# Twenty-four modulation vectors made in the attention stage instead of the mixing stage

## The chip, the cores and the metric

The kernel runs on one core of a Trainium2 chip. The metric is device time in microseconds for one execution of the whole program, as the median of several executions. The core's engines are TensorE (PE, with its weight loads shown apart as PEld), VectorE (DVE), ScalarE (ACT), GpSimd (POOL) and SyncE (SP), which here only issues DMAs. Each engine works through its own queue in order.

## The reference, cut to what matters

Two post-norm layers run over 1024 latent and 128 context tokens of width 1024. Each layer first makes six modulation vectors of width 1024 from a condition vector, one set for latent tokens (`c`) and one for context tokens (`c_ctx`):

```python
mod = (jax.nn.silu(cvec) @ lp['w_mod'] + lp['b_mod'])[:, None, :]
sh1, sc1, g1, sh2, sc2, g2 = jnp.split(mod, 6, axis=-1)
h = x * (1 + sc1) + sh1
... = jnp.split(h @ lp['w_in'] + lp['b_in'], offsets, axis=-1)
a_out, mla_st = mla_mixer(...)     # 8 attention heads
m_out, ml_st = mlstm_mixer(...)    # 4 heads, matrix memory, both directions
g_out, hg_st = hgrn_mixer(...)     # 4 heads, gated linear recurrence, both directions
mix = jnp.concatenate([a_out, m_out, g_out], axis=-1) @ lp['w_out']
x = layernorm(ALPHA * x + g1 * mix, lp['ln1_g'], lp['ln1_b'])
h2 = x * (1 + sc2) + sh2
gate, up = jnp.split(h2 @ lp['w_ffn_in'], 2, axis=-1)
x = layernorm(ALPHA * x + g2 * ((jax.nn.silu(gate) * up) @ lp['w_ffn_out']), ...)
```

`sh1` and `sc1` are needed at once; `g1`, `sh2` and `sc2` only behind the output projection of the three mixers, and `g2` at the end of the layer.

## The kernel before

In the kernel the 6 x 1024 modulation values of a layer are 48 vectors of 128 values, numbered j = 0 to 47, kept for both conditions in `modfm`. Vectors 0 to 15 are `sh1` and `sc1`, 16 to 23 `g1`, 24 to 31 `sh2`, 32 to 39 `sc2`, 40 to 47 `g2`. One vector is made by `mod_gemv` (line 209): a DMA of 512 KB brings its 128 x 1024 weights, and for each of the two conditions one DVE instruction (`scalar_tensor_tensor`, line 213) multiplies them with the condition's row, which stands in all 128 partitions (`cB`), and sums along the row; the product itself goes to a scratch tile (`junk`). In the trace each of the two shows as a SCALAR_TENSOR_TENSOR and a short DVE_READ_ACCUMULATOR. `mod_init` loads the two rows by a broadcasting DMA, `mod_bias` (line 220) adds the bias for eight vectors, and `gsave` (line 225) transposes eight finished vectors on PE and stores them, from where `gbcast` reads a gate row later.

A layer is four stages, run one behind the other by `run`:

- `phase_a`, the mixing stage: input projection and the two recurrences. The gated recurrence (`hgrn_setup`) works on blocks of 384 tokens; the mLSTM (`ml_gates`, `ml_states`, `mlstm`) on nine chunks of 128 tokens. `mla_prep` normalises the low-rank query and key streams and spills them.
- `phase_b`, attention: weights are split into a high and a low part, keys, values and queries of head 0 are made, then 152 steps run, 8 heads x 19 steps, of which a head has one for the context tokens and nine for each half of the latent tokens. A step is three score matmuls (lines 1182 to 1184), the exponential and the high part on ACT (1185, 1186), the low part on POOL (1187), and two steps later three matmuls with the values (1255 to 1257). Between them, two pieces per step from a list `todo`: the maxima of the next head's scores (`peak`, matmul on line 1136 and a DVE reduction on line 1137), and its keys, values and queries. In heads 6 and 7 the list has `rec` (line 1222 on), which multiplies the two recurrences' outputs with their gates (line 1229) and transposes them.
- `phase_c`, output projection and first layer norm; `phase_d`, the feed-forward.

`mm3` (lines 155 to 157) makes a product of full precision out of three matmuls of split operands, and `split` (150, 151) and `unit` (145, 146) make such operands: a cast on ACT and a subtraction on DVE or POOL.

In the kernel before, layer 0 makes its vectors 16 to 39 in `phase_a`, by `start_mod`: eight between the steps of the gated recurrence's input projection and of `mla_prep`, sixteen between the chunks of `mlstm`, with two weight buffers, two condition rows and a scratch tile of their own in each place. Vectors 40 to 47 are made in the feed-forward stage (`ffn_in`), and layer 1's 48 in layer 0's `ffn_out`. Lines 1283 to 1292, which could make vectors from 40 on in attention's last heads, do nothing, since their counter starts at 40 and runs to 40.

In layer 0 `mlstm` scales its output rows on POOL (lines 865 and 876), in layer 1 on DVE (`LG`).

The program's text doesn't fix the order on an engine alone: the tile framework plans it with a model of time (`schedule_with_timeline_sim=True`), takes work that stands later in the text ahead when its operands are there, and sets the semaphores. A tile's memory is taken over from earlier tiles at the same place, and the first instruction on it waits for their last use. In `phase_b` the calls `ze([P, 328])` and `ze([P, 576])` take memory that nothing uses.

## Time and profile before

| | us |
|---|---|
| median of 3 executions | 3640.34 (3639.33 to 3640.81) |
| the profiled execution | 3641.28 |
| its span, first to last instruction | 3639.5 |
| PE busy | 3405.9 (94%) |
| DVE busy | 2264.8 (62%) |
| POOL busy | 1988.8 (55%) |
| ACT busy | 1635.7 (45%) |
| mean granted clock of PE | 0.953 of full speed |

All times in the rows below are microseconds from the span's start. In a view by stretch each row has the stretch, its length, the busy time of PE, PEld, DVE, ACT and POOL with the number of instructions, the granted PE clock, the busy share of the DMA engines and GB/s. In a view of groups each row has line, engine, operation, operands with their shapes, the count, then after the bar the busy time, the mean duration in ns, and the idle time of the engine just before them with what ended it. In a timeline a row has start, duration, engine, line and operation, with idle time before it in brackets. L213 is line 213 of the kernel; a PE that is called busy may still be waiting inside, since the ends of pipelined matmuls are modelled.

### The profile page before, as it was taken

The page shows a single profiled execution, that of the slowest core. Times are in us where ns is not written, and L with a number is a line of the kernel's source. Part 1 is how long each engine was busy: PE and PEld are TensorE (multiplying, and loading weights), DVE is VectorE, ACT ScalarE, POOL GpSimd, SP SyncE. Part 2 cuts the span into 40 slices and gives each one's busy share as a digit, 9 for nine tenths or more (in the row PEclk, how much of TensorE's full clock was granted, in tenths as well). Part 3 has the DMA queues.
Part 4 walks back from the last instruction along what each step waited for, and adds up shares of the span by engine and source line. Part 5 has one row for each costly group of instructions (what it writes and reads, how often), then busy time and mean ns, then how long its engine had stood idle before and what let it go on. Part 6 is the DMA issues. An engine that isn't in the chain of part 4 may idle for free. (4 is left out here: it accounts for less than half of the span.)

```text
span 3639.5 us, 56085 instructions
## 1 busy us (share of the span) xinstructions
PE 3405.9 (94%) x20556; PEld 3034.6 (83%) x20556; DVE 2264.8 (62%) x4492; ACT 1635.7 (45%) x2877; POOL 1988.8 (55%) x1745
## 2 busy tenths in 40 slices
PE   7999987999989999999889989989999999999997
PEld 7998875776779999988689888877767899998875
DVE  6868878555674444487775678765558544443246
ACT  4264564887343333312272636577853433333211
POOL 3455566777665555401453556567863555552176
PEclk9899976999989999999999999789999999999998
DMA  6212153002352222375422021401044322224222
GB/s 244 72 40 43 39 167 100 18 21 81 121 160 85 85 85 85 111 252 179 156 79 62 30 45 34 137 25 25 22 132 139 110 73 73 73 74 139 94 99 80
DMA packets 331272, 335.77 MB, mean 92 GB/s; under 512 B 191458, under 2 KB 270386, under 8 KB 330996
## 3 DMA queue, kind: packets, MB, share of 16 engines
q1 hardware_dynamic: 330996, 332.19, 29.5%
q8 instruction: 161, 2.64, 0.3%
q14 instruction: 115, 0.94, 0.1%
HBM read 263.54 MB, written 68.56 MB: 91 GB/s over the span
## 5 line engine op out<-in xcount | busy, mean ns | idle before, releaser
L151 POOL TENSOR_TENSOR t<-t,t 128x512 fp32r<-128x512 f32 (+3 forms) x318 | 437.8, 1378 | 374.8 <-ACT t L150 374.4
L150 ACT CAST t<-t 128x512 fp32r<-128x512 f32 (+5 forms) x404 | 270.7, 673 | 698.0 <-PE bank L1449 278.7
L1449 PE MATMUL bank<-hhi,t 128*128 128x256 f32 (+1 forms) x2816 | 570.8, 295 | 12.4 <-DVE t L1349 11.5
L155 PE MATMUL bank<-hhi,t 128*128 128x384 f32 (+1 forms) x1220 | 455.1, 378 | 19.2 <-ACT t L150 5.1
L157 PE MATMUL bank<-hhi,t 128*128 128x384 f32 (+1 forms) x1220 | 460.0, 378 | 8.8 <-DVE t L151 8.8
L1449 PEld LDWEIGHTS bank<-hhi,t 128*128 128x128 f32 x2816 | 456.2, 189 | 13.6 <-ACT t L150 12.3
L156 PE MATMUL bank<-hlo,t 128*128 128x384 f32 (+1 forms) x1220 | 460.9, 378 | 4.9 <-POOL hlo L151 4.1
L1187 POOL TENSOR_TENSOR t<-t,t 128x512 fp32r<-128x512 f32 (+1 forms) x304 | 383.3, 1281 | 125.4 <-ACT t L1186 103.0
L1449 PE MATMUL bank<-t,t 128*128 128x320 f32 (+1 forms) x3168 | 434.2, 297 | 2.3 <-DVE t L1507 1.7
L1449 PEld LDWEIGHTS bank<-t,t 128*128 128x128 f32 x3168 | 427.9, 190 | 3.7 <-DVE t L1507 1.9
L1449 PE MATMUL bank<-hlo,t 128*128 128x320 f32 (+1 forms) x1408 | 415.2, 295 | 0.0
L155 PE MATMUL bank<-t,hhi 128*128 128x256 f32 (+3 forms) x1232 | 386.8, 315 | 12.1 <-DVE t L1107 5.4
L156 PE MATMUL bank<-t,hhi 128*128 128x256 f32 (+3 forms) x1232 | 388.0, 315 | 4.3 <-POOL t L146 4.3
L157 PE MATMUL bank<-t,hlo 128*128 128x256 f32 (+3 forms) x1232 | 388.4, 316 | 0.3 <-POOL hlo L151 0.3
L155 PEld LDWEIGHTS bank<-hhi,t 128*128 128x128 f32 x1220 | 237.9, 196 | 57.3 <-ACT t L150 6.7
L1137 DVE TENSOR_REDUCE t<-bank 128x1 f32<-128x384 f32 (+1 forms) x400 | 203.9, 538 | 122.6 <-PE bank L1136 119.5
L157 PEld LDWEIGHTS bank<-hhi,t 128*128 128x128 f32 x1220 | 240.1, 197 | 39.2 <-DVE t L151 12.1
L156 PEld LDWEIGHTS bank<-hlo,t 128*128 128x128 f32 x1220 | 239.6, 196 | 34.7 <-POOL hlo L151 5.1
L1449 PEld LDWEIGHTS bank<-hlo,t 128*128 128x128 f32 x1408 | 265.4, 188 | 0.3 <-issue 0.2
L155 PEld LDWEIGHTS bank<-t,hhi 128*128 128x128 f32 x1232 | 239.8, 195 | 30.2 <-DVE t L1107 5.6
L213 DVE SCALAR_TENSOR_TENSOR t<-t,t 128x1024 bf16<-128x1024 f32 x176 | 239.3, 1359 | 40.6 <-DMA t<-in_w_mod_dram 31.6
L156 PEld LDWEIGHTS bank<-t,hhi 128*128 128x128 f32 x1232 | 240.4, 195 | 20.1 <-POOL t L146 4.7
(355 smaller groups left out, 7329.1 us busy)
## 6 DMA issues: line engine op xcount, KB each, us to landing
t<-in_w_mod_dram SPq DMA_DIRECT2D x96, 512.0 KB
t<-in_w_ffn_in_dram SPq DMA_DIRECT2D x88, 512.0 KB
t<-in_w_ffn_out_dram SPq DMA_DIRECT2D x44, 512.0 KB
t<-in_w_in_dram SPq DMA_DIRECT2D x40, 512.0 KB
shid<-t SPq DMA_DIRECT2D x88, 160.0 KB
sx<-t SPq DMA_DIRECT2D x27, 512.0 KB
t<-sx SPq DMA_DIRECT2D x27, 512.0 KB
shid<-t SPq DMA_DIRECT2D x88, 128.0 KB
```

The costliest lines, as they stand in the source:

```text
L150: self.nc.scalar.copy(hi, src)
L151: (eng or self.nc.gpsimd).tensor_tensor(lo, src, hi.bitcast(F32), op=ALU.subtract)
L155: mm(ps, a[0], b[0], start=first, stop=False)
L156: mm(ps, a[0], b[1], start=False, stop=False)
L157: mm(ps, a[1], b[0], start=False, stop=last)
L213: nc.vector.scalar_tensor_tensor(junk, raw, 1.0, cB[s], op0=ALU.mult, op1=ALU.mult, accum_out=self.modfm[:, l, j, s:s + 1])
L1137: V.tensor_reduce(nm[:, i, b:b + 1] if i < 8 else nm[:, i, 3:4], ps, axis=AX.X, op=ALU.max, negate=True)
L1187: G.tensor_tensor(pl, e, ph.bitcast(F32), op=ALU.subtract)
L1449: mm(ps, a[x][:, k * P:(k + 1) * P], view(y, k, n0, n1), start=first and k == 0 and i == 0, stop=k == 3 and i == 2, skip_group_check=True)
```

## The change

Vectors 16 to 39 of layer 0 are made in `phase_b` of layer 0 and no longer in `phase_a`: from step 3 to step 95 of attention, one after every fourth step. There is one weight buffer (`rv`), which layer 0 alone allocates. The two condition rows take two tiles of 128 x 1024, and the rings `rr` and `rg` of `rec` become four slices of 256 of the same two tiles (before: three tiles of 256 each). The scratch tile takes the place of `ze([P, 576])`, till now unused. To make room, the two one-row tiles for the softmax denominators become rows 0 and 32 of one tile. `start_mod` and the lines that did nothing go.

```diff
-    def start_mod(self, z, j0, j1):
-        raw = z.ring(2, [P, U])
-        cB, junk = [z([P, D]), z([P, D])], z([P, D], BF16)
-        self.mod_init(cB)
-
-        def gen():
-            for j in range(j0, j1):
-                self.mod_gemv(0, j, cB, raw.next(), junk)
-                if j % 8 == 7:
-                    self.mod_bias(0, j - 7, 8)
-                if j == 23:
-                    self.gsave(0, 16, self.r_m.next())
-                yield
-
-        return gen()
...
-                        bg = self.start_mod(Zone(self, c, "gemv"), 16, 24) if l == 0 else iter(())
+                        bg = iter(())
...
-                bg = self.start_mod(zl, 24, 40) if l == 0 else iter(())
+                bg = iter(())
...
-            ze([P, 576])
+            junk = ze([P, 576]).bitcast(BF16)[:, 0:D]
...
-            rdn = z.ring(2, [1, QB])
-            rr, rg = z.ring(3, [P, 256]), z.ring(3, [P, 256])
+            dn = z([33, QB])
+            rdn = Ring([dn[0:1, :], dn[32:33, :]])
+            cB = [z([P, D]) for _ in range(2)]
+            rr, rg = [Ring([a[:, 256 * i:256 * (i + 1)] for i in range(4)]) for a in cB]
+            if l == 0:
+                rv = z.ring(1, [P, U])
...
-            todo, gj = [], [40]
+            todo, mods = [], list(range(16, 40))
...
-                if l == 0 and n == 6 * 19 + 6 and gj[0] < 40:
-                    cB = [wks[:, i, :].bitcast(F32) for i in range(2)]
+                if l == 0 and n == 0:
                     self.mod_init(cB)
-                    junk = wqs.tiles[0].rearrange("p a b -> p (a b)").bitcast(BF16)
-                if l == 0 and n >= 6 * 19 + 7 and n%2==1 and gj[0] < 40:
-                    j = gj[0]
-                    gj[0] += 1
-                    self.mod_gemv(0, j, cB, rU.tiles[j % 2][:, 0:U], junk)
+                if l == 0 and n % 4 == 3 and mods:
+                    j = mods.pop(0)
+                    self.mod_gemv(0, j, cB, rv.next(), junk)
                     if j % 8 == 7:
                         self.mod_bias(0, j - 7, 8)
+                    if j == 23:
+                        self.gsave(0, 16, r_p.next())
```

## Rows read from the trace of the kernel before

**Rows 1.** The page: busy time per engine, and 40 slices of the span.

```profile
PE 3405.9 (94%) x20556; PEld 3034.6 (83%) x20556; DVE 2264.8 (62%) x4492; ACT 1635.7 (45%) x2877; POOL 1988.8 (55%) x1745
...
PE   7999987999989999999889989989999999999997
...
PEclk9899976999989999999999999789999999999998
```

**Rows 2.** Busy time by stretch: from:to, length, PE, PEld, DVE, ACT, POOL, clock, DMA.

```profile
80.00:100.00 20.00, 15.07 (x86) 14.34 (x85) 20.00 (x35) 6.65 (x9) 9.01 (x6) 0.74 0.41 142
...
120.00:140.00 20.00, 14.06 (x93) 13.45 (x92) 19.96 (x50) 6.05 (x10) 16.35 (x14) 0.80 0.22 62
481.40:614.90 133.50, 95.73 (x453) 80.39 (x452) 121.04 (x329) 53.29 (x119) 94.75 (x96) 0.67 0.51 158
2287.30:2394.90 107.60, 90.00 (x454) 79.47 (x454) 91.11 (x294) 59.56 (x143) 55.10 (x65) 0.68 0.41 122
614.90:813.90 199.00, 193.58 (x943) 152.34 (x942) 109.43 (x215) 163.66 (x319) 147.68 (x121) 0.98 0.08 18
813.90:929.30 115.40, 105.43 (x475) 75.98 (x475) 67.40 (x131) 89.42 (x173) 86.43 (x67) 0.96 0.29 80
```

**Rows 3.** Busy time by stretch of line 213 alone, on DVE.

```profile
74.00:132.00 58.00, 21.08 (x32) 0.91 0.31 104
481.40:557.40 76.00, 25.38 (x37) 0.74 0.60 181
557.40:614.90 57.50, 18.96 (x28) 0.59 0.39 126
1060.00:1500.00 440.00, 26.81 (x32) 1.00 0.30 89
```

**Rows 4.** Waits, 74:140: who waited for whom, us in total, times, longest.

```profile
PE bank L156 <- POOL t L146: 4.3, 2, 3.7
PE bank L225 <- DVE modfm L220: 4.2, 1, 4.2
```

**Rows 5.** Groups by line in 481.4:614.9: count | busy us, mean ns | idle.

```profile
L213 DVE SCALAR_TENSOR_TENSOR t<-t,t 128x1024 bf16<-128x1024 f32 x32 | 44.1, 1377 | 5.7 <-DMA t<-in_w_mod_dram 3.7 <-DMA t<-scr 1.9
...
L865 POOL TENSOR_TENSOR t<-t,t 128x256 f32<-128x256 f32 x18 | 17.2, 976 | 7.5 <-DVE t L862 6.8 <-DVE modfm L220 0.5
```

**Rows 6.** Groups by line in layer 1's 2287.3:2394.9.

```profile
L876 DVE TENSOR_TENSOR t<-t,t 128x256 f32<-128x256 f32 x18 | 9.8, 551 | 0.1
...
L865 DVE TENSOR_TENSOR t<-t,t 128x256 f32<-128x256 f32 x18 | 8.1, 494 | 0.0
```

**Rows 7.** Groups by line in 614.9:813.9, layer 0's attention.

```profile
L1187 POOL TENSOR_TENSOR t<-t,t 128x512 fp32r<-128x512 f32 x90 | 116.8, 1316 | 33.7 <-ACT t L1186 29.3 <-PE bank L1257 1.6 <-ACT t L1185 1.3
L1137 DVE TENSOR_REDUCE t<-bank 128x1 f32<-128x384 f32 x115 | 60.5, 550 | 45.2 <-PE bank L1136 44.7
...
L1128 DVE CAST t<-hlo 32x1152 fp32r<-32x1152 f32 x5 | 6.8, 1355 | 1.0 <-PE bank L1182 0.8
...
L1108 DVE TENSOR_TENSOR t<-t,t 128x384 f32<-128x384 f32 x3 | 5.8, 1934 | 0.0
...
L151 DVE TENSOR_TENSOR t<-t,t 64x1152 fp32r<-64x1152 f32 x3 | 5.3, 1765 | 1.2 <-ACT t L150 1.1
```

**Rows 8.** Timeline of DVE in attention, 690:702.

```profile
695.23 4.33 DVE L1108 TENSOR_TENSOR t<-t,t 128x384 f32<-128x384 f32 x1
```

**Rows 9.** Timeline of POOL, the same stretch.

```profile
694.96 1.30 POOL L151 TENSOR_TENSOR hlo<-t,hhi 128x512 fp32r<-128x512 f32 x1
696.21 2.93 POOL L1187 TENSOR_TENSOR t<-t,t 128x512 fp32r<-128x512 f32 x3
```

**Rows 10.** Timeline of PE, the same stretch.

```profile
700.09 0.33 PE L1136 MATMUL bank<-t,t 96*128 96x128 f32 x1 [2.61 <-DVE t L1137]
```

**Rows 11.** Busy time by stretch, in layer 0's feed-forward input.

```profile
1100.00:1150.00 50.00, 50.00 (x379) 50.00 (x378) 23.83 (x38) 15.44 (x32) 31.00 (x27) 1.00 0.29 87
```

**Rows 12.** Timeline of DVE near 560: start us, duration us, line, operation.

```profile
560.55 0.63 DVE L1229 TENSOR_TENSOR t<-t,t 128x256 f32<-128x256 f32 x1
```

## The prediction

> **What bounds the kernel now.** I read the page first. The tensor engine (PE) is busy for 94% of the span [rows 1], so the kernel is bound by PE wherever PE's slice shows a 9, and work on VectorE (DVE) costs time only where PE's slice falls. The reader is to see the two kinds of place where it falls beside a lower granted clock: in slice 1, at the start, and in slices 6 and 7, where the recurrences end and attention begins and the granted clock is 7 and 6 tenths (in layer 1 that place is slices 26 and 27, at 7 and 8).
>
> Then I read busy times by stretch, with edges taken from the trace: 481.4 is the end of the last gated-recurrence output, 614.9 the first softmax exponential of attention. This stretch, which I call the transition, takes 133.5 us in layer 0 with DVE busy for 121.0 of them, PE for 95.7 at a granted clock of 0.67 [rows 2]. Layer 1 runs the same stretch without modulation vectors in 107.6 us [rows 2]. So DVE is what is late in layer 0's transition, and 25.9 us stand between the two layers.
>
> Line 213 alone says where the moved work sits. One vector is two halves, each one multiply with a sum (scalar_tensor_tensor) and one read of the accumulator: 4 instructions. The 24 moved vectors stand in two places [rows 3]: 8 of them (32 instructions, 21.1 us) in 74 to 132, and 16 in the transition, 37 instructions in its mLSTM part and 28 in its last 57.5 us (one on the edge counts twice). The other eight of layer 0's later vectors run under the feed-forward product and stay.
>
> Where the work goes, steps 0 to 95 of layer 0's attention (614.9 to 813.9), PE is busy for 193.6 of 199.0 us, POOL for 147.7, ScalarE for 163.7 and DVE for 109.4 [rows 2]. PE is the bound there, but two others are not far behind.
>
> **The change, part by part.**
>
> *Eight vectors leave the start.* DVE is busy for all of 80 to 100 and 120 to 140, where PE idles 4.9 and 5.9 us [rows 2]. Of these 10.9 us, 4.3 are PE waiting for POOL's split of a weight, line 146, which is no gemv; 4.2 are PE's transposition of the eight finished vectors (line 225), waiting for their bias [rows 4]. I take 10.9 less 4.3 = 6.6 us as the gain; ends 0 (something else is late in the same places) and 10.9 us.
>
> *Sixteen vectors leave the transition.* They take 25.4 + 19.0 = 44.3 us of DVE there [rows 3]. Without them DVE has 121.0 - 44.3 = 76.7 us of work, less than layer 1's 91.1 in 107.6 us [rows 2]. What is late next is POOL: layer 0 leaves the two row scalings of the mLSTM output on POOL (lines 865 and 876; 865 alone takes 17.2 us) where layer 1 has them on DVE at 8.1 and 9.8 us [rows 5, 6]. POOL has 94.8 us in layer 0's transition [rows 2]. So 107.6 us is the floor, a gain of 25.9, and I take 20: 113.5 us, in which POOL's 94.8 fit. The other end is 5 us, if POOL's queue is what the first attention step waits for.
>
> *Twenty-four vectors enter attention,* one after every fourth step, 3 to 95. Each brings a DMA of 512 KB on SP's queue, two DVE halves and, after each eighth, one bias. The price of a vector on DVE is 21.08 / 8 = 2.64 us at its least and 26.81 / 8 = 3.35 us beside POOL's work [rows 3], so 63 to 80 us. DVE's 109.4 + 63 = 172 us still fit into 199, and 109.4 + 80 = 189 just. Cover by count alone is there; whether it holds is the question, since DVE's queue is in order and the reductions of the score peaks (115 full ones of 0.55 us [rows 7]) that free PE's banks stand behind a gemv half.
>
> The price that decides is met in the trace at 695.23: a DVE product of two SBUF tensors, line 1108, took 4.33 us [rows 8], against a smallest share of the same form of about (5.8 - 4.33) / 2 = 0.7 us [rows 7]. POOL ran four instructions without a break from 694.96 to 699.14 [rows 9], and DVE's instruction ended right after them. PE, whose banks wait for the reduction queued behind it, stood for 2.61 us [rows 10]. A gemv half is of this kind too: two SBUF tensors in.
>
> The Trainium skill, "SBUF — State Buffer", section "Who interferes with whom", states that a DVE instruction with two SBUF inputs contends with a GpSimd instruction that reads SBUF, and that whoever has the shared ports keeps them for its whole instruction. By that rule, the trace agrees at this place (4.33 us), and it speaks against the change.
>
> As a mechanism of this kernel: if the gemv halves and POOL's instructions take turns, the 199.0 us must hold POOL's 147.7 us and 24 x 2.64 = 63.4 us one after the other, 211.1 us in all, which is 12.1 us too many. I add 2 us for half of the transposition's 4.2 us wait [rows 4], which moves here too (line 225 now takes one of the three banks of attention's ring), and take +14 us. The low end is 0: in the feed-forward product, eight vectors run beside POOL at 31.0 of 50 us and PE stays at 50.00 [rows 3, 11]. The high end is the price paid in the transition: 25.9 us for 16 vectors is 1.6 us each, 39 us for 24.
>
> *The queues that it is moved past.* SP issues 24 loads more in attention; with one buffer each waits for the gemv before. Behind it on SP stand the small round trips of the softmax sums, which are due four and more steps (8 us) later, so a wait of one gemv is covered. The DMA engines are busy for 0.08 there [rows 2]; 24 x 512 KB over 199 us is 63 GB/s beside 18. In the transition the two loads of the silu rows and sixteen of weights go away; DVE's own waits for them there were 5.7 us [rows 5], and lie within the gain.
>
> *Shared memory.* The buffers of the gated recurrences' tail (rings r and g) go from three to four entries and hold the gemv's rows until step 95; their first use in order is in head 6, step 116, so nothing waits by count. Today the first of their products runs at 560 already [rows 12], well ahead; in layer 0 this is no longer possible, and they run where PE idles 10.0 of 115.4 us [rows 2]. I take 0, within 3 us either way. The denominators now lie in one tile of two rows; a row is reused two blocks of nine steps later. Nothing.
>
> *The sum.* -6.6 - 20 + 14 = -12.6 us. The profiled execution took 3641.28 us (span 3639.5 and 1.8 around it), 0.94 above the median of 3640.34. So 3641.3 - 12.6 = 3628.7 there, and 3628 for the median.
>
> **The rivals.**
>
> *Attention hides it all.* For it: PE at 50.00 in the feed-forward stretch [rows 11], and DVE idle for 89.6 of 199.0 us [rows 2]. Against it: in the feed-forward product PE waits for DVE seldom, in attention every peak waits for a reduction. Time: 3641.3 - 26.6 - 0.9 = 3614.
>
> *The halves and POOL block each other, and PE pays as in the transition* (slower). Place: steps 0 to 95. Price: 1.6 us per vector, 39 us; -26.6 + 39 = +12.4, so 3653. It decides from 26.6 / 24 = 1.1 us per vector on; my +14 is 0.58. For it: 4.33 us and PE's 2.61 [rows 8, 10], and the sum of 211 over 199. Against it: the eleven SBUF-only instructions of the like that attention has on DVE in these steps (five casts, six products) average 1.6 us [rows 7], and PE idles only 5.4 us over all of them [rows 2].
>
> *The transition stays as long.* The kernel's order comes from a planner that pulls ready work ahead: a product that is written for head 6 stands at 560, 54 us ahead of attention's first step [rows 12]. It may pull the first new vectors back into 557 to 615, as soon as their memory is free, or POOL's 94.8 us may bound it. Gain there 5 instead of 20: -6.6 - 5 + 14 = +2.4, so 3643. The change then does only part of what it says. Against it: layer 1's 107.6 us with more DVE work than layer 0 will have [rows 2].
>
> **How the numbers follow.** Forecast 0.42 (3618 to 3638), all hidden 0.14, blocked 0.22, transition stays 0.22. A measurement of this kernel can tell about 0.2%, 7.3 us, from no change: 3633 to 3648 is "same". Faster: four fifths of the forecast, the hidden case and a little of the last, 0.49; slower: the blocked case and a quarter of the last, 0.27; same: the rest, 0.24. The likeliest is 3628. With the blocked case's 3653 and bounds of the unknown costs about it, and the hidden case's 3614, the range is 3607 to 3660.
>
> **What the changed profile would show.** Right: no line 213 between 74 and 615 but the first eight's; 80 to 140 with PE idle under 5 us; the last recurrence output to the first exponential in 110 to 118 us; steps 0 to 95 in 208 to 218 us with gemv halves above 1.4 us on average and PE waiting for line 1137 more than today's. Wrong: gemv rows ahead of the first exponential, a transition above 125 us, steps 0 to 95 within 3 us of 199 (hidden) or above 230 (blocked). Layer 1's stretches should stand within 3 us.

## The result, and the profile after

The changed kernel took 3664.23 us, median of 5 executions (3656.29 to 3670.05), beside 3640.81 (3639.33 to 3651.36) of the kernel before: a ratio of 1.0054 [1.0030, 1.0078] (ratios weigh all executions; the two medians alone would give 1.0064). Run again later (`after_again`, expected below) it took 3663.28 beside 3646.26, 1.0050 [1.0033, 1.0068]. The forecast was 3628, its range ended at 3660. The profiled execution has a span of 3667.5 us, 28.0 more than before.

The page of the changed kernel, which answers to [rows 1]:

```profile
PE 3426.9 (93%) x20556; PEld 3049.5 (83%) x20556; DVE 2283.6 (62%) x4492; ACT 1640.2 (45%) x2879; POOL 1998.2 (54%) x1745
...
PE   8999997899979999999899989989989899999997
...
PEclk9999967999989999999999999789999999999998
```

The sums hardly move; what moves is where PE idles. The first slice rises from 7 to 8. Slices 6 and 7 (455 to 637 us) stood at 8 and 7; now slices 7 and 8 (550 to 734 us) stand at 7 and 8, and those hold the end of the transition and the first two thirds of attention's steps 0 to 95. The stretches of the changed kernel, in the columns of [rows 2]. Lines have moved: 1187 is now 1175 (POOL's subtraction), 1137 is 1125 (the reduction of a peak), 1136 is 1124, 1257 is 1245 (the last product with the values), 1219 is 1207 (POOL's scaling by the softmax sums).

```profile
80.00:100.00 20.00, 17.45 (x146) 16.67 (x146) 17.13 (x33) 13.97 (x18) 11.47 (x13) 1.00 0.09 27
120.00:140.00 20.00, 20.00 (x178) 19.87 (x178) 16.07 (x65) 3.63 (x8) 8.32 (x9) 1.00 0.23 68
458.50:579.60 121.10, 101.09 (x461) 88.52 (x460) 92.41 (x279) 60.62 (x143) 83.44 (x101) 0.61 0.43 132
579.60:822.70 243.10, 213.20 (x932) 159.46 (x932) 171.83 (x300) 164.46 (x318) 172.50 (x121) 0.91 0.20 60
822.70:935.70 113.00, 101.90 (x475) 74.82 (x475) 71.40 (x131) 89.08 (x172) 87.72 (x66) 0.97 0.25 74
2304.50:2421.60 117.10, 98.85 (x454) 87.22 (x453) 95.16 (x296) 59.80 (x142) 55.30 (x65) 0.66 0.40 117
```

80 to 100 and 120 to 140 idle for 2.6 us in place of 10.9. The last gated-recurrence output comes at 458.5, not 481.4; the transition takes 121.1 us in place of 133.5; steps 0 to 95 take 243.1 in place of 199.0, which is more than both gains together; behind step 95 the stretch is 2.4 us shorter. POOL, which has the same 121 instructions there, is busy for 172.5 us in place of 147.7. Layer 1's transition takes 117.1 us in place of 107.6.

Of the 28.0 us between the two profiles only 9.8 stand at the end of layer 0's output projection (1044.1 in place of 1034.3, the start of the last instruction that takes up its products). The other 18.2 come behind it, in work that the change leaves alone; in the profile of `after_again` it is 9.0 and 17.4. The experiments on the memory come back to this.

A stretch can be split, as an estimate, by its own row: PE's busy time times the granted clock is the work at full speed, the rest of its busy time is what the clock took, and length less busy is idle. Steps 0 to 95 were 189.7 + 3.9 + 5.4 [rows 2]; now they are 194.0 + 19.2 + 29.9. The work is nearly the same; 24.5 us more are idle and 15.3 us more went with the clock.

Groups by line in that stretch, changed kernel (answering to [rows 7]):

```profile
L1175 POOL TENSOR_TENSOR t<-t,t 128x512 fp32r<-128x512 f32 x90 | 133.0, 1502 | 42.0 <-ACT t L1174 33.5 <-PE bank L1172 5.0 <-PE bank L1245 3.4
L213 DVE SCALAR_TENSOR_TENSOR t<-t,t 128x1024 bf16<-128x1024 f32 x37 | 66.7, 1801 | 23.9 <-DMA t<-in_w_mod_dram 23.8
L1125 DVE TENSOR_REDUCE t<-bank 128x1 f32<-128x384 f32 x118 | 61.7, 547 | 22.8 <-PE bank L1124 22.0
```

A half takes 1.80 us on average (1.38 in the transition before [rows 5]); 90 POOL subtractions take 1.502 in place of 1.316; and DVE stood for 23.8 us waiting for the weights of the next vector. The reductions keep their 0.55. Matched one by one in the trace, 35 of the 90 subtractions met a half and took 1.82 us on average, the other 55 took 1.30; of all 48 moved halves, nine met no POOL instruction and took 1.20 to 1.23 us, the other 39 took 1.79 on average. What PE and POOL stood for there (who waited for whom, us in total, times, longest; `sri` brings the softmax sums back by SP's queue):

```profile
PE bank L1124 <- DVE t L1125: 10.9, 6, 3.9
PE bank L1245 <- POOL t L1175: 7.6, 10, 1.5
POOL t L1175 <- ACT t L1174: 49.5, 17, 16.0
POOL t L1207 <- DMA t<-sri: 12.5, 4, 6.6
```

The two waits of PE were 2.6 and 0.3 us before. How the two slow each other, on three engines' timelines:

```profile
698.10 2.11 DVE L213 SCALAR_TENSOR_TENSOR t<-t,t 128x1024 bf16<-128x1024 f32 x1 [1.06 <-DMA t<-in_w_mod_dram]
...
700.61 1.81 DVE L213 SCALAR_TENSOR_TENSOR t<-t,t 128x1024 bf16<-128x1024 f32 x1
```

```profile
699.08 4.47 POOL L1175 TENSOR_TENSOR t<-t,t 128x512 fp32r<-128x512 f32 x2
```

```profile
701.39 0.45 PE L1245 MATMUL bank<-t,t 128*65 128x512 f32 x1 [0.85 <-POOL t L1175]
...
703.61 0.44 PE L1245 MATMUL bank<-t,t 128*65 128x512 f32 x1 [0.67 <-POOL t L1175]
```

Two subtractions next to two halves took 4.47 us, 2.2 each, and PE waited for both. That is the other direction of [rows 8 to 10], where DVE was the one held up.

### The profile page after: what moved, and what is told of

Its sections match the earlier page's. It is cut to its first block, busy times and chain, and to the rows that moved or that the text cites. A ratio compares the mean times of both kernels' runs of the same rounds, so it can differ in the third digit from the quotient of the medians.

```text
span 3667.5 us, 56098 instructions
## 1 busy us (share of the span) xinstructions
PE 3426.9 (93%) x20556; PEld 3049.5 (83%) x20556; DVE 2283.6 (62%) x4492; ACT 1640.2 (45%) x2879; POOL 1998.2 (54%) x1745
## 5 line engine op out<-in xcount | busy, mean ns | idle before, releaser
L1175 POOL TENSOR_TENSOR t<-t,t 128x512 fp32r<-128x512 f32 (+1 forms) x304 | 407.8, 1362 | 147.1 <-ACT t L1174 117.4
L213 DVE SCALAR_TENSOR_TENSOR t<-t,t 128x1024 bf16<-128x1024 f32 x176 | 255.1, 1450 | 54.2 <-DMA t<-in_w_mod_dram 51.6
```

The lines of the kernel that those rows point to most:

```text
L213: nc.vector.scalar_tensor_tensor(junk, raw, 1.0, cB[s], op0=ALU.mult, op1=ALU.mult, accum_out=self.modfm[:, l, j, s:s + 1])
L1175: G.tensor_tensor(pl, e, ph.bitcast(F32), op=ALU.subtract)
```

## The experiments

The theories: **P**, a half and POOL's instructions hold one another up; **Q**, DVE's queue is simply too full, whatever POOL does; **D**, with one weight buffer the load comes late and DVE's queue stands behind it; **S**, the loads cost by their place on SP's queue or in the DMA engines; **M**, the changed memory costs. Ratios are to the kernel before on the same chip, with 95% intervals; one per cent is 36 us.

| run | time, us | ratio | steps 0 to 95 |
|---|---|---|---|
| before | 3640 to 3646 | 1 | 199.0 |
| after_again | 3663.28 | 1.0050 [1.0033, 1.0068] | 241.9 |
| no_vectors | 3612.17 | 0.9913 [0.9890, 0.9936] | 199.4 |
| loads_only | 3601.42 | 0.9888 [0.9867, 0.9908] | 194.3 |
| one_input | 3643.29 | 0.9994 [0.9982, 1.0006] | 213.3 |
| short_loads | 3659.88 | 1.0052 [1.0033, 1.0072] | 229.0 |
| quarters | 3658.54 | 1.0040 [1.0024, 1.0057] | 235.6 |
| sixteen_moved | 3651.30 | 1.0017 [1.0003, 1.0030] | 222.6 |
| eight_moved | 3651.59 | 1.0022 [1.0006, 1.0037] | 203.6 |
| rings_only | 3648.85 | 1.0019 [1.0008, 1.0031] | 196.2 |
| after_old_rings_l1 | 3654.55 | 1.0035 [1.0021, 1.0049] | 240.6 |
| eight_old_rings_l1 | 3645.60 | 1.0005 [0.9992, 1.0018] | 205.8 |
| start_later | 3644.11 | 0.9995 [0.9984, 1.0006] | 204.3 |
| start_out | 3638.33 | 0.9989 [0.9978, 0.9999] | 209.1 |
| start_loads_only | 3640.76 | 0.9988 [0.9974, 1.0002] | 211.1 |
| start_short_loads | 3641.50 | 1.0000 [0.9992, 1.0009] | 196.4 |
| start_pinned | 3631.47 | 0.9977 [0.9962, 0.9991] | 194.5 |
| start_pinned_again | 3638.07 | 0.9977 [0.9965, 0.9990] | 194.0 |
| start_pinned_cq | 3644.63 | 0.9996 [0.9983, 1.0010] | 198.6 |

The last column is one profiled execution each, first exponential to that of step 96. Steps 0 to 95 of a kernel like before spread over 194 to 211 us there, so only differences above that say something.

**The changed kernel once more.**

> The changed kernel itself once more, beside the kernel before on this chip, so that the other runs of this group have a figure taken under the same conditions. Expected: 3655 to 3666, a ratio of 1.003 to 1.007.

As expected; in its profile, steps 0 to 95 and the subtraction's mean (1.501) repeat to 1.2 us and 0.001 us.

**What the vectors cost, and whether it is the loads.** `no_vectors`:

```diff
+        nc.vector.memset(self.modfm[:, 0, 16:40, :], 0.0)
...
-                rv = z.ring(1, [P, U])
...
-                    self.mod_init(cB)
...
-                    self.mod_gemv(0, j, cB, rv.next(), junk)
```

> The changed kernel with the 24 vectors left out wholly (no loads, no DVE halves; the values are set to zero, so layer 0's first gate and second modulation are wrong). It is the floor for all that follows. All theories expect: attention's steps 0 to 95 of layer 0 back at 199 us within 4 (243.1 in the changed kernel), DVE's transition work near 77 us and the transition at 105 to 112 us, total 3590 to 3602. If instead steps 0 to 95 stay above 215, the new rings or the shared denominators cost the time and not the vectors.

`loads_only` keeps the loads and drops the halves:

```diff
...
-                    self.mod_gemv(0, j, cB, rv.next(), junk)
+                    nc.sync.dma_start(rv.next(), ins["w_mod"][0, j])
```

> The changed kernel with the 24 loads of weights and the two rows kept, but without the DVE halves (values set to zero). Theory P (halves and POOL block each other on what they share), theory Q (DVE's queue is simply longer) and theory D (DVE's queue stands still until the late load has landed, 23.8 us in the changed kernel) all expect the floor within 5 us, since nobody waits for the loads: 3590 to 3605. Theory S (SP's queue and the transfers themselves hold up attention) expects 10 us or more above the floor.

```profile
566.90:766.30 199.40, 194.48 (x951) 151.51 (x950) 113.07 (x225) 166.15 (x323) 148.40 (x121) 0.99 0.08 18
```

That row is steps 0 to 95 of `no_vectors`: they are back at 199.4 us. Against it the changed kernel's vectors cost 1.0050 - 0.9913, 50 us, 2.1 us a vector (with both intervals some 10 us either way). The time, 3612, is 10 us above what all theories expected. With the loads alone nothing is lost (0.9888; by that floor the vectors would cost 59 us), so the loads by themselves cost nothing. But none of these loads waits for a half to free its buffer; for that part of S see `short_loads`.

**One SBUF input in place of two.** Each half becomes a plain sum of the weights, with one SBUF input and as many columns (and without the product tile that a half writes):

```diff
-                    self.mod_gemv(0, j, cB, rv.next(), junk)
+                    raw = rv.next()
+                    nc.sync.dma_start(raw, ins["w_mod"][0, j])
+                    for s in range(2):
+                        V.tensor_reduce(self.modfm[:, 0, j, s:s + 1], raw, axis=AX.X, op=ALU.add)
```

> The changed kernel with each DVE half replaced by a sum over the weight row alone (tensor_reduce, one input from SBUF instead of two, some 1.2 us like the half at its least; the product with the condition is left out). Loads, buffers and places are kept. Theory P expects POOL's subtraction (line 1175) back at 1.32 us from 1.50, the sums at 1.2 us instead of the halves' 1.80, and steps 0 to 95 at 205 to 215 us, total 3600 to 3615. Theory Q expects 235 to 245 us for these steps and 3645 to 3660 in all. Theory D expects the waits for loads to stay above 15 us and steps 0 to 95 at 222 to 232 us, total 3625 to 3640.

The durations in ns, min/median/max, of the 48 instructions of the changed kernel and of this one, then this one's steps 0 to 95 and its group of POOL's subtractions:

```profile
L213 DVE SCALAR_TENSOR_TENSOR t<-t,t x48: 1202/1528/5092, 526.4 to 727.2; 128x1024 bf16<-128x1024 f32 x48
```

```profile
L1278 DVE TENSOR_REDUCE modfm<-t x48: 1167/1209/1221, 470.0 to 642.3; 128x1 f32<-128x1024 f32 x48
```

```profile
584.20:797.50 213.30, 201.25 (x934) 154.82 (x933) 130.69 (x240) 164.74 (x320) 147.49 (x121) 0.94 0.14 39
```

```profile
L1175 POOL TENSOR_TENSOR t<-t,t 128x512 fp32r<-128x512 f32 x90 | 117.0, 1318 | 51.3 <-ACT t L1174 33.5 <-PE bank L1172 12.5 <-PE bank L1244 3.5
```

At their least the two cost the same (1.17 and 1.20 us). With one input none of 48 takes more than 1.221, though 44 of them ran beside a POOL instruction, and the 14 subtractions that met a sum took 1.28 us on average. With the matching of the changed kernel's own instructions above, it is shown that a half and POOL's instructions stretch one another: P. That it comes from the second SBUF input rather than from the product that a half writes as well, two other DVE products of the changed kernel suggest (450 to 930 us; `bank` is one of the banks that PE writes its results to, `t` lies in SBUF; ns, min/median/max):

```profile
L1095 DVE TENSOR_TENSOR t<-bank,t x12: 515/542/557, 533.7 to 700.1; 128x384 f32<-128x384 f32 x12
L1217 DVE TENSOR_TENSOR t<-t,t x18: 404/648/2248, 731.7 to 923.7; 128x256 f32<-128x256 f32 x18
```

The first has one SBUF input and writes a wider result, eleven of twelve times beside POOL, and never stretches; the second has two and does.

What the stretching costs is not isolated by this run. The planner set 29 of the 48 sums ahead of the first exponential (of the halves 11), so that 19 stand in steps 0 to 95 in place of 37; POOL's mean of 1.318 is in part that. And DVE waits there 9.0 us for weights in place of 23.8. By time the two-input form, and what moved with it, is 1.0050 - 0.9994 = 20 us of the 50; 3643 is well above the 3600 to 3615 that P forecast. The other 30 us (0.9994 - 0.9913) remain with one input: Q and D, of which the profile has 13.9 in steps 0 to 95 and 16.9 in the transition (126.1 us beside the 109.2 of `no_vectors`).

**The late load.** `short_loads` fills the buffer once and cuts the 24 loads to 32 KB (the product is made with what the buffer holds):

```diff
+                nc.sync.dma_start(rv.tiles[0], ins["w_mod"][0, 16])
...
-                    self.mod_gemv(0, j, cB, rv.next(), junk)
+                    raw = rv.next()
+                    nc.sync.dma_start(raw[:, 0:64], ins["w_mod"][0, j][:, 0:64])
...
```

> The changed kernel with the loads of the 24 vectors cut to 64 of 1024 columns (32 KB instead of 512 KB; the other columns stay those of vector 16, so layer 0's second set of values is wrong), halves and places kept. Theory D (DVE's queue stands still for a late load, 23.8 us in the changed kernel) expects these waits below 8 us and attention's steps 0 to 95 at 215 to 225 us, total 3635 to 3645. Theory P (halves and POOL block each other) expects the halves still above 1.6 us, POOL's subtraction above 1.45 us and the steps at 232 to 245 us, 3650 to 3665, unless the plan puts the halves elsewhere.

```profile
L1176 POOL TENSOR_TENSOR t<-t,t 128x512 fp32r<-128x512 f32 x90 | 132.2, 1492 | 47.3 <-ACT t L1175 34.4 <-PE bank L1173 9.2 <-PE bank L1245 3.7
...
L1279 DVE SCALAR_TENSOR_TENSOR t<-t,t 128x1024 bf16<-128x1024 f32 x34 | 61.3, 1804 | 5.7 <-DMA t<-in_w_mod_dram 5.5
```

DVE's wait for the weights falls from 23.8 to 5.5 us, halves and subtractions stay as slow (1.804, 1.492), and steps 0 to 95 shorten by 14 us (with 34 halves in them in place of 37). Yet the time doesn't fall beyond its uncertainty (1.0052 beside 1.0050), where D had forecast 3635 to 3645. D is real in the profile and small, or given back, in the time. The rest of S goes with it: SP still stands 45.3 us behind halves that hold the buffer (36.6 in the changed kernel), and POOL's wait for the softmax sums (12.5 us above, 2.3 before) is gone, without a gain in time.

`quarters` does the same product from two loads of 256 KB each in two half buffers, with 96 instructions of 512 columns:

```diff
-                rv = z.ring(1, [P, U])
+                rv, mx = z.ring(2, [P, U // 2]), z([P, 8, 2])
...
-                    self.mod_gemv(0, j, cB, rv.next(), junk)
+                    for q in range(2):
+                        raw, cs = rv.next(), slice(512 * q, 512 * q + 512)
+                        nc.sync.dma_start(raw, ins["w_mod"][0, j][:, cs])
+                        for s in range(2):
+                            V.scalar_tensor_tensor(junk[:, cs], raw, 1.0, cB[s][:, cs], ...
...
```

> The changed kernel with each vector in two loads of 256 KB into two buffers of half the size, and each half in two quarters of 512 columns (96 instructions in place of 48, the two sums added for eight vectors at once). The same product is computed. Theory D (a vector waits for its load, since there is one buffer, and the reductions of the peaks wait behind it): the loads are hidden, steps 0 to 95 take about 229 us in place of 243, 3645 to 3654. Theory P with short holds (a quarter lets a reduction in sooner, and waits for POOL only as much in all): steps 0 to 95 below 222, 3638 to 3648. Rival (each instruction waits for POOL anew, so twice as many instructions wait twice as often): quarters above 1.1 us on average, steps 0 to 95 at 243 or more, 3660 to 3675.

```profile
L1279 DVE SCALAR_TENSOR_TENSOR t<-t,t x96: 647/843/2029, 517.1 to 696.9; 128x512 bf16<-128x512 f32 x96
```

A quarter takes 0.65 us at its least and 1.03 on average, so 96 of them take 98.5 us of DVE, where the 48 halves of the changed kernel take 81.0 (58 at their least): each instruction waits anew, as the rival has it, though less at a time (it expected above 1.1 us). Steps 0 to 95 at 235.6 and 3658.54 lie between the theories, and the interval overlaps the changed kernel's: no gain is shown.

**Fewer vectors.** `sixteen_moved` leaves 16 to 23 at the start and sets 24 to 39 after every sixth step:

```diff
-                        bg = iter(())
+                        bg = self.start_mod(Zone(self, c, "gemv"), 16, 24) if l == 0 else iter(())
...
-            todo, mods = [], list(range(16, 40))
+            todo, mods = [], list(range(24, 40))
...
-                if l == 0 and n % 4 == 3 and mods:
+                if l == 0 and n % 6 == 5 and mods:
```

> The changed kernel with the vectors 16 to 23 back at the start as in the kernel before, and only 24 to 39 in attention, one after every sixth step. Theory P (a half and the POOL subtraction hold one another up, about 1.8 us a vector) gives steps 0 to 95 in 215 to 230 us, a transition of 115 to 125 us and a start as before: 3641 - 12 + 24 + 6 for the shared memory = about 3659, between 3648 and 3664. Rival Q (the loss comes from too many vectors in the 96 steps and falls away at the slower pace): steps 0 to 95 in 200 to 210 us, and 3636 to 3645.

```profile
588.50:811.10 222.60, 206.23 (x945) 158.96 (x945) 148.61 (x269) 164.76 (x320) 163.83 (x121) 0.93 0.17 47
```

222.6 us, as P has it, with 11.0 idle and 10.5 of clock more than before. `eight_moved` moves 16 to 23 alone, after every twelfth step, and `mlstm` keeps its sixteen:

```diff
-                bg = iter(())
+                bg = self.start_mod(zl, 24, 40) if l == 0 else iter(())
...
-            todo, mods = [], list(range(16, 40))
+            todo, mods = [], list(range(16, 24))
...
-                if l == 0 and n % 4 == 3 and mods:
+                if l == 0 and n % 12 == 11 and mods:
```

> Only vectors 16 to 23 move into attention, one after every twelfth step; 24 to 39 are made between the mLSTM chunks as before. In the changed kernel the start is 23 us shorter up to the last gated-recurrence output, and a vector in attention costs 44 / 24 = 1.8 us. If both hold one by one: 3641 - 23 + 8 x 1.8 = 3632. If the price is lower for vectors that stand further apart (theory P, where a half hits a POOL that has idle time in between): 0.5 us each, 3622. If the start's gain is lost again on the way (by other work that was planned behind it): 3640 or more.

There steps 0 to 95 took only 203.6 us, since the planner ran all 48 halves (16 moved, 32 of `mlstm`) between 470 and 632, 38 of them ahead of the first exponential, so that the transition stayed as long as before (134.5 us). The pace written in the text does not bind. The time is what the third expectation has (3640 or more).

**The memory.** `rings_only` is the kernel before with the new rings and the denominators' tile alone:

```diff
-            rdn = z.ring(2, [1, QB])
-            rr, rg = z.ring(3, [P, 256]), z.ring(3, [P, 256])
+            dn = z([33, QB])
+            rdn = Ring([dn[0:1, :], dn[32:33, :]])
+            cB = [z([P, D]) for _ in range(2)]
+            rr, rg = [Ring([a[:, 256 * i:256 * (i + 1)] for i in range(4)]) for a in cB]
...
```

> The kernel before with the memory part of the change alone: denominators as two rows of one tile, and the rings r and g as four slices of two shared tiles. The vectors are made where they were. In the changed kernel, and in all four variants run so far, layer 1 (whose work is the same) takes 2 to 19 us longer than in the kernel before, most of it between step 133 of attention and the end of the output projection and in the mLSTM part. Theory M (the memory part costs it): layer 1 longer by 8 to 12 us, 3648 to 3654 in all. The other theory (a shifted plan and the spread between executions, nothing of the memory): within 4 us of the kernel before.

`after_old_rings_l1` is the changed kernel with those lines for layer 0 and the old two for layer 1:

```diff
+            if l == 0:
...
+            else:
+                rdn = z.ring(2, [1, QB])
+                rr, rg = z.ring(3, [P, 256]), z.ring(3, [P, 256])
```

> The changed kernel with the shared memory in layer 0 alone; layer 1 has its three-entry rings and two denominator tiles as before. Theory M expects 8 to 12 us less than the changed kernel's 3660, so 3648 to 3652. The other theory expects 3656 to 3664.

The memory costs 0.19%, 7 us (3 to 11). The changed kernel is about as much faster without it in layer 1, but 3654.55 lies between the two expectations and its interval overlaps the changed kernel's. Where: step 133 to the end of the output projection, layer 1, in the kernel before, the changed one and `after_old_rings_l1`:

```profile
2662.80:2811.30 148.50, 142.60 (x645) 111.65 (x646) 113.86 (x194) 63.86 (x114) 63.91 (x44) 0.99 0.43 130
```

```profile
2690.40:2847.20 156.80, 146.38 (x651) 113.63 (x650) 114.99 (x194) 65.16 (x117) 64.64 (x44) 0.97 0.41 126
```

```profile
2684.80:2833.50 148.70, 141.69 (x645) 110.41 (x646) 112.67 (x194) 63.76 (x114) 65.35 (x44) 1.00 0.43 130
```

A wait for shared memory is not what does it. `start_out` below has the old memory and takes 157.2 us for this stretch, while `start_pinned` takes 148.5. Over all twenty profiles, the eight in which PE's instructions there follow each other as in the kernel before take 148.0 to 152.8 us; the twelve in which they come in another order, two of them with the old memory, take 152.9 to 158.1. The planner carries an edit in layer 0 on into layer 1's order. That the order, rather than the memory behind it, costs this stretch its 6 to 8 us is argued from these profiles; no run fixed the order alone, and the stretch is only part of what `rings_only` loses behind layer 0's output projection (13.6 us in its profile).

`eight_old_rings_l1` is `eight_moved` with the old rings in layer 1:

```diff
...
+            else:
+                rdn = z.ring(2, [1, QB])
+                rr, rg = z.ring(3, [P, 256]), z.ring(3, [P, 256])
```

> Only vectors 16 to 23 in attention, one every twelfth step, and the shared memory in layer 0 alone. With eight vectors moved, layer 0 ended 10 us earlier than in the kernel before and layer 1 took 14 us longer. Theory M expects layer 1 back and 3630 to 3634, faster than both kernels. The other theory expects 3645 to 3652 as with the shared memory in both layers.

A miss: no faster than before. It counted on the start's 22.9 us, which the next runs take apart.

**What the start was worth.** `start_later` is the kernel before without the call of `next(bg, None)` in the first projection, so that the eight vectors are written behind it.

```diff
                             V.tensor_tensor(v[:, tt, :], ps, br, op=ALU.add)
-                            next(bg, None)
```

> The kernel before, one edit: the eight vectors 16 to 23 are no longer issued one for each tile of the first value projection (74 to 132 us) but one for each of the next eight tiles, the latent projections. No vector enters attention and no memory changes. Theory A (the start was dear because the eight vectors filled VectorE in 80 to 140, which let TensorE idle and its granted clock fall to 0.74 to 0.80): the last output of the gated recurrences comes 10 to 20 us earlier than the 481.4 of before, the rest keeps its length, and the time is 3622 to 3635. Rival B (the eight vectors cost the start about their own length wherever they stand before the recurrences): 3638 to 3646, no change.

It tells nothing of A or B: the sixteen halves still ran between 74 and 130, where the planner had them. `start_out` leaves them out, `start_loads_only` keeps their loads, `start_short_loads` keeps the halves and cuts six of the loads:

```diff
+        nc.vector.memset(self.modfm[:, 0, 16:24, :], 0.0)
...
-                self.mod_gemv(0, j, cB, raw.next(), junk)
+                if j >= 24:
+                    self.mod_gemv(0, j, cB, raw.next(), junk)
```

> The kernel before with the vectors 16 to 23 left out (not computed, taken as zero ahead of their bias); all else, the memory too, as before. It gives the whole price of the eight at the start. Expected if the 22.9 us of the changed kernel's start are these vectors': the last output of the gated recurrences near 459 in place of 481, and about 3620 (3614 to 3628). If part of it came from the changed memory or order: 3628 to 3640.

```diff
...
+                else:
+                    self.nc.sync.dma_start(raw.next(), self.ins["w_mod"][0, j])
```

> The kernel before with the eight loads of 512 KB kept at the start and their sixteen halves left out (taken as zero). Theory V (the price is VectorE's 21 us of halves in front of other work): as without the vectors, 3614 to 3628, TensorE's granted clock near 1.00 in 80 to 140. Theory L (the price is the loads, which stand on SyncE's queue and in the DMA engines ahead of the weights): 3634 to 3646, and the clock in 80 to 140 as in the kernel before.

```diff
...
+                    w = raw.next()
...
+                        self.nc.sync.dma_start(w[:, 0:64], self.ins["w_mod"][0, j][:, 0:64])
...
```

> The kernel before with the sixteen halves kept at the start and six of the eight loads cut to 32 KB (the product is made with what the buffer holds). Theory V: as before, 3638 to 3646. Theory L: 3616 to 3630.

Without the eight, 80 to 140 has PE at 57.1 of 60 us:

```profile
80.00:140.00 60.00, 57.09 (x491) 55.73 (x490) 43.67 (x149) 22.49 (x34) 30.86 (x30) 1.00 0.18 50
```

Before it was 49.1 at a clock of 0.85. The first gated-recurrence output comes 25.3 us earlier (214.6 in place of 239.9), but the last one only 8.4 earlier (473.0), and layer 0's output projection ends 5.0 us earlier (1029.3 in place of 1034.3; `rings_only`, which moves no vector, has 1029.7, so this says little). By time it is 0.11% [0.01, 0.22], 4 us. So a stage boundary that comes 25 us sooner was worth 4; where the rest went is not shown. In the profiles DVE is the price, as theory V says: with the loads alone PE's clock in 80 to 140 is at 1.00, with the halves and short loads it stays at 0.85. In the time the intervals of the three (0.9989, 0.9988, 1.0000) overlap, and of the size that V gave (3614 to 3628) nothing is left.

`start_pinned` has the edit of `start_later` and ties each load behind a latent-projection tile by a one-column copy into its buffer; `start_pinned_cq` takes the query's projection, one stage later:

```diff
...
+            self.pin = y[:, 0:1]
             next(bg, None)
...
+                w = raw.next()
+                if j < 24:
+                    self.nc.vector.tensor_copy(w[:, 0:1], self.pin)
+                self.mod_gemv(0, j, cB, w, junk)
```

> The kernel before with the eight vectors tied to the latent projections: one column of the weight buffer is written from that projection's result ahead of each load, so that the load, and the halves behind it, come after it (about 140 to 200 us, where VectorE is busy for 45 of 60 us). The same product is computed. Theory A (the eight are dear at 74 to 132 because VectorE is full there): the last output of the gated recurrences 8 to 20 us earlier than 481.4, and 3622 to 3634, below both kernels. Rival B (they cost their length wherever they stand ahead of the recurrences): 3638 to 3650.

> The version with the eight vectors tied to the latent projections once more. If the 0.23% holds: a ratio of 0.996 to 0.999, 3626 to 3637. If it was chance: 0.999 to 1.001.

> The same with the eight tied to the query's latent projection, the stage behind (about 165 to 210 us). The same product is computed. Theory A (they are cheapest where VectorE is not full, and PE has its work): 3624 to 3634. Rival (each place ahead of the recurrences costs its stage about the same idle time of TensorE): 3634 to 3645.

`start_pinned` beats both kernels, the one before by 0.23% in two groups of runs. But A's reason isn't what its profile shows: the last gated-recurrence output stands at 481.3, as before, and the idle time has moved with the vectors:

```profile
80.00:140.00 60.00, 56.76 (x473) 54.56 (x472) 46.16 (x134) 24.76 (x34) 28.74 (x27) 1.00 0.28 84
140.00:180.00 40.00, 29.77 (x209) 27.06 (x208) 36.60 (x106) 7.49 (x13) 23.75 (x29) 0.83 0.27 83
```

Layer 0's output projection ends at 1033.8 and, in the repeat, 1030.8 (before: 1034.3). Where the 8 us come from stays open. One stage later nothing is gained.

## Why the prediction was wrong, point by point

The step that failed is the sum of attention: what two engines need one after the other was laid against the length of the steps, and only what stood out over it, 12.1 us, was charged. The runs showed 44 us there, and 50 by time.

**The start, -6.6, and the transition, -20: together too small.** Leaving all 24 vectors out on the same memory (`no_vectors` beside `rings_only`, 0.9913 and 1.0019) is worth 39 us by time, some 9 either way, where the two terms gave 26.6 and at most 36.8. How it divides is open. Leaving the start's eight out alone saves 4 us, within my 0 to 10.9; the sixteen would then be worth 35, if the two add. By the two profiles they do not: 18.1 us stand ahead of the last gated-recurrence output, 23.5 in the transition. So the -6.6 came near what the eight are worth alone, but not for its reason: the idle time of 80 to 140 did go, and the time followed by less than the first boundary's 25.3 us.

The floor of the transition was well chosen, since without vectors it takes 109.2 us (107.6 in layer 1 [rows 2]). I held its edge, 481.4, fast, and the edge moves: with the sixteen gone (`sixteen_moved`, start unchanged) it comes at 468.4, 13.0 us earlier, or 7.4 earlier than the 475.8 of `rings_only`, which moves no vector. In the changed kernel itself the transition gained 12.4 of the 20 us: its 121.1 still have 11 of the 48 halves in them, which the planner pulled ahead of the first exponential, as the third rival said that it might.

**Attention, +14: the step that made it wrong.** It cost 44 us in steps 0 to 95, and 50 by time for the 24 vectors wherever the plan set them, above my high end of 39 (by time only just clear of it); steps above 230 us were the prediction's own sign of the blocked rival. The sum put 147.7 us of POOL and 63.4 of halves one after the other and so counted all of POOL's 51.3 idle us as room for halves. That room was not there. Counted in the changed kernel's trace, POOL's instructions and the 37 halves that came into the steps cover 186.1 us, 38.4 more than POOL alone before, where 37 halves at their least take 44; and for 57.0 us neither ran, 5.7 more than before. POOL's idle time there is mostly waiting for ACT (49.5 us above, 33.4 before), and a half that is ready at another moment does not fill it. So it is the halves' own time, and not what stands out over 199.0, that was added.

Three things go into that. Both sides stretch: 37 halves take 66.7 us and 90 subtractions 133.0 in place of 116.8 [rows 7]; `one_input`, which ends this and moves some of the sums elsewhere, gave 20 us back. A fuller DVE costs by itself: with instructions of a steady 1.21 us (`one_input`) the vectors still cost 30 us by time, late loads and a transition of 126.1 us among it, though by count DVE had room (130.7 of 213.3 us busy). The prediction called this cover by count, and gave it no price of its own. And PE's idle time came with a lower granted clock, 0.91 for 0.98, which took another 15 us by the estimate above, and which no term of the sum held. How much of the 50 us is the first and how much the second, no run here separates cleanly.

By the Trainium skill, "SBUF — State Buffer", section "Who interferes with whom", which the prediction weighed, a DVE instruction with two SBUF inputs contends with a GpSimd instruction that reads SBUF, for ports that only one of them can hold. The trace agrees: 1.21 us with one input, up to 5.09 with two, and subtractions of 1.82 us where they met a half and 1.30 where not. That the holder keeps the ports for its whole instruction stands there beside other DVE modes; which of the two held them, the trace does not tell. The prediction had looked for the wait on DVE; here POOL and, behind it, PE paid too.

**SP's queue, nothing: right in the time**, by `loads_only` and `short_loads`. In the profile the cover of one gemv did not hold: SP stood 36.6 us behind halves, and POOL 12.5 us for softmax sums, longest 6.6, where it was 2.3 before. The one buffer was passed over: DVE waited 23.8 us for weights. Without either wait (`short_loads`) the steps are 14 us shorter in the profile, and the time, within uncertainty, the same.

**Shared memory, 0 within 3: wrong by size**, 7 us (3 to 11), and wrong by place: layer 1, whose stretches were to stand within 3 us. In the profiles 18.2 of the changed kernel's 28.0 us stand behind layer 0's output projection, and `rings_only` loses 13.6 there; 8.0 are left when layer 1 has the old memory (`after_old_rings_l1`, whose layer 0 ends 5.6 us later than the changed kernel's). No term of the sum had a place for this.

**The sum.** By time: -39 + 50 + 7 = +18; measured +17 to +23. This closes by construction, since the three are differences between kernels that lie one behind the other from the one before to the changed one; it is no test. The rival that the halves and POOL block each other (3653) named the mechanism and came nearest; its loss of 39 was short of 50 and its gain of 26.6 short of 39, which offset one another: that it came so near in time is in part luck. Against it I had held that PE idles only 5.4 us beside eleven instructions of the like; eleven in 199 us were no measure for the 37 halves that came.

## What to carry to other kernels

Where a two-input DVE instruction is moved beside a busy POOL, price both as stretched, each by the other, and add what PE loses in granted clock once it idles in pieces. Don't count the other engine's idle time as room: it waits for something then, and a sum of lengths that just fits is already a loss. Don't book a stage boundary that comes earlier as a gain: with an order that a planner makes, only the time tells (25 us at one boundary were 4), and an edit in one layer can change the order in the next. To move work for certain, give it a dependency; its place in the text moved nothing in `start_later` and set no pace in `eight_moved`.

## What the hardware showed that was not expected

The same 1024 columns take 1.167 to 1.221 us with one SBUF input, 44 of 48 of them beside POOL, and 1.202 to 5.092 with two. POOL's subtraction, a 128x512 instruction, slows from 1.316 to 1.502 us on average, and two beside halves took 4.47. A DVE product with one input from PE's banks did not stretch beside POOL (line 1095, 0.52 to 0.56 us). But one SBUF input is no safeguard for every operation: the cast on line 1116 took 0.75 us where it met no POOL instruction and 1.08 to 2.00 where POOL ran beside it:

```profile
L1116 DVE CAST t<-hlo x8: 752/1249/2001, 560.7 to 814.5; 32x1152 fp32r<-32x1152 f32 x8
```

PE's mean granted clock went from 0.98 to 0.91, a mix of its two levels of 1.2 and 2.4 GHz, while PE was still busy for 213.2 of 243.1 us; its waits in that stretch were up to 3.9 us long.
